# Feed-forward of a decoder layer: the three partial products of a block, ordered by part instead of by slice

## The chip, the cores and the metric

The kernel runs on one core of a Trainium2 chip. Its engines have queues of their own and meet by semaphores: TensorE (PE in the profile, PEld for its weight loads), VectorE (DVE), ScalarE (ACT), GpSimd (POOL) and SyncE (SP, which issues the DMAs). The metric is the device time of one execution in microseconds (us), as the median of the runs.

## The reference

One decoder layer on a sequence of 1024 tokens with width 1024. The change lies in its second half, the gated feed-forward:

```python
D_FF = -(-8 * D_MODEL // (3 * 256)) * 256          # 2816

def swiglu(h, w_gate, w_up, w_down):
    return (jax.nn.silu(h @ w_gate) * (h @ w_up)) @ w_down

def reference(...):
    ...
    x = layer_norm(ALPHA * x + gate1 * mix, ln1_g[l], ln1_b[l])
    h = x * (1.0 + scale2) + shift2
    ffn = swiglu(h, w_gate[l], w_up[l], w_down[l])
    x = layer_norm(ALPHA * x + gate2 * ffn, ln2_g[l], ln2_b[l])
    return x
```

All arrays are float32. The first half (modulation, projections, sparse attention, pooling, output projection, first norm) is the same in both kernels.

## The kernel before

**Numbers in two parts.** TensorE multiplies in a float32 form that rounds its operands. To keep precision, every operand is split into a high part (a rounded copy, made by ScalarE) and a low part (the operand less its high part, a subtraction on VectorE or GpSimd). A tile holds the high part in its columns 0 to 511 and the low part in 512 to 1023. A product of two operands is then three matmuls added up in PSUM, in the order of a table of pairs (part of the first operand, part of the second):

```python
SPLITS = ((0, 0), (0, 1), (1, 0))     # high by high, high by low, low by high
```

**Seven products in place of eight.** Each of the three feed-forward products of a pair of 128-column blocks is done as a two by two block product with seven block products (sums and differences of quarters are formed ahead, by GpSimd for weights and mostly by VectorE for activations). So gate, up and down consist of seven steps each. In `gu_step(kind, n, ...)` (`kind` "g" or "u", `n` 0 to 6) the weight block is the stationary operand and the tokens `TOK` (profile: `hr_H`) the moving one; the twelve matmuls of a step (four slices `k` by three pairs) accumulate in one PSUM bank, `gu`. In `down_step(p, n)` the activations `ACTS` (`act_W`, `act_R`) are stationary and the weight block moves; here the twelve matmuls are four row groups `i` by three pairs, and each row group has its own bank, `dn`, of the four banks of pool `ps3`.

**Weight blocks.** A block passes through GpSimd (sums, or a product with the gate row) in `wraw_R` or `wraw_W`, ScalarE (the high part) and VectorE or GpSimd (the low part) into one of four ring buffers: two in region V (`wblk_V`), two in region T (`wblk_T`). The raw sets come in by DMA; the next load is issued when a low part has been taken.

**Order.** The second half is written out by hand and kept in program order on TensorE, VectorE, ScalarE and GpSimd. A period `p` (1 to 9) has the steps of `DOWN_AT = 'dgggdggdggddduuduuuuu'`; below they are called d0 to d6, g0 to g6 and u0 to u6. So d3, d4 and d5 follow one another with nothing between them; all other down steps have gate or up steps in between. The last period has gate and up steps alone, and the last two down products are done by `last_down`.

**What is evacuated, and when.** The down step's banks are added to the residual (`res_X`) by four VectorE additions, one for each bank, right behind the step in VectorE's queue (`adds`). A table says which step begins new banks and which goes on in the banks of the step before (d1 in d0's, d3 in d2's, d5 in d4's; the additions take the bank's sum both times):

```python
DOWN = (("A11", "B11", True, (22,)), ("A12", "B21", False, (11,)), ("S1", "T1", True, (22,)), ("A22", "T4", False, (-21,)),
        ("S3", "T3", True, (22,)), ("S4", "B22", False, (-12,)), ("S2", "T2", True, (22,)))
```

New or not, a step's first matmul into a bank comes after the addition that read this bank before. In period 1 the first step's banks are copied by ScalarE and d1, d3 and d5 use a scaled addition in place of the plain one.

All engine calls go through one helper, so nearly every row of the profile says L174; the rows are told apart by their tiles.

Of the kernel before, what the change touches and what calls it, by code (L numbers as in the profile page):

```python
# [73 lines left out]
def f_(ap):  # L74

    return ap.bitcast(F32)


class Times:
# [11 lines left out]
    def place(self, ap):  # L91
        if ap.name in self.prev or ap.name in self.psum:
            p = self.psum.setdefault(ap.name, [np.zeros(2), np.full(2, " "), np.zeros(2), np.full(2, " ")])
            o = ap.offset % 1024
            return p, slice(o // 512, (o + ap.shape[-1] - 1) // 512 + 1) if len(ap.shape) == 2 else slice(0, 2)
        rng = getattr(ap.tensor, "manual_sbuf_range", None)
        if rng is None:
            return None
        es = {F32: 4, F32R: 4, I32: 4}.get(ap.dtype, 2)
        dims = list(ap.ap)  # L100
        lo = ap.offset % dims[0][0] if dims[0][0] else ap.offset
        hi = lo
        for st, n in dims[1:]:
            if st < 0:
                lo += st * (n - 1)
            else:
                hi += st * (n - 1)
        g = self.GRAIN
        return self.sbuf, slice((rng[0] + es * lo) // g, (rng[0] + es * hi) // g + 1)
# [77 lines left out]
def decoder_layer_kernel(  # L187
# [30 lines left out]
    def ps_tile(pool, tag, n, depth, nm):  # L218
        n_ps[0] += 1
        t = pool.tile([P, n], F32, tag=tag, name=f"{nm}_{n_ps[0]}")  # L220
        ring = ps_ring[tag]
        times.prev[t[:, 0:n].name] = ring[-depth] if len(ring) >= depth else None
        ring.append(t[:, 0:n].name)
        return t

    def psA(nm="pa"):
        return ps_tile(ps1, "ps1", 512, 4, nm)
# [65 lines left out]
    SPLITS = ((0, 0), (0, 1), (1, 0))  # L293
# [826 lines left out]
    for n_, u in enumerate(units):  # L1120
        g, pr, i = u
# [171 lines left out]
    def block(n):  # L1293
        if n < 8:
            return FIRST[n]
        if n < len(blocks) - 8 or n >= len(blocks) - 4:
            return RING[n % NRING]
        return TOK[:, 1, n + 8 - len(blocks)]
# [96 lines left out]
    def gu_step(kind, n, i0, ni, act, halves=True, turned=0):  # L1395


        gu_blk[n] = pos["used"] + (n if i0 + ni < 4 else n == 4 and halves)
        j = slice(i0 * P, (i0 + ni) * P)
        if n in (0, 1, 3):  # L1400
            gu_bank["ADxB"[n]] = psA("gu")[:, 0 : ni * P]
        banks = dict(gu_bank)
        ps_ = banks["ADABAAD"[n]]

        def mm(out_, m_, ks, new):
            w_, b = block(gu_blk[m_]), STEPS[m_][1]
            pv = out_.rearrange("p (i q) -> p i q", q=P)
            for k in ks:
                for m, (x, y) in enumerate(SPLITS):
                    T.matmul(pv, w_[:, x * 512 + k * P : x * 512 + (k + 1) * P], TOK[:, i0 : i0 + ni, b, y * 512 + k * P : y * 512 + (k + 1) * P],  # L1410
                             start=(new and k == 0 and m == 0), stop=(k == 3 and m == 2), skip_group_check=True)

        mm(ps_, n, range(2 if n == 3 and halves else 4), n in (0, 1, 3))
        if n == 4 and halves:
            mm(banks["B"], 3, (2, 3), False)

        gt = [GTMP[3 * turned], GTMP[1], GTMP[2], GTMP[3 - 3 * turned]]
        t1, t2, t4 = (x[:, j] for x in ((gt[0], gt[1], gt[3]) if kind == "g" else UTMP))
        outs = {4: ((3, t4), (0, t1)), 5: ((1, ps_),), 6: ((2, t2),)}.get(n, ())
        place = lambda q: gt[(0, 2, 1, 3)[q]]  # L1420
        sl = Slot()
        sl.used = ((1, 1, 1, 0, 2, 1, 1)[n] if halves else 1) if i0 + ni == 4 else 0

        def copy():
            if n in (0, 2, 4):
                A.activation((t1, None, t2, None, t4)[n], ps_, AF.Copy)

        def vec():
            for q, val in outs:
                if n == 4:  # L1430
                    V.tensor_tensor(val, val, banks["D" if q == 3 else "B"], ALU.add)
                elif n == 6:
                    V.tensor_tensor(val, val, ps_, ALU.add)
                if kind == "u":
                    V.tensor_tensor(place(q)[:, j], place(q)[:, j], val, ALU.mult)
            if kind == "u" and n == 5 and type(act) is dict:
                V.tensor_tensor(UTMP[0], place(1), place(3), ALU.add)

        def high(nm_, src):
            x = act[nm_]  # L1440
            A.activation(x[:, 0:512], src, AF.Copy)
            pend_low.append(lambda: (G if nm_ in ACT_G else V).tensor_tensor(x[:, 512:1024], src, f_(x[:, 0:512]), ALU.subtract))

        def sums():
            if kind == "u" and type(act) is dict:
                g11, g12, g21, g22 = gt
                todo_ = {5: (("S3", UTMP[2], g11, g21),), 6: (("S2", UTMP[0], UTMP[0], g11), ("S4", UTMP[1], UTMP[0], g12))}.get(n, ())
                for nm_, dst, x, y in todo_:
                    (G if nm_ in SUM_G else V).tensor_tensor(dst, x, y, ALU.subtract)
                    pend_high.append(lambda nm_=nm_, dst=dst: high(nm_, dst))  # L1450

        def act_():
            for q, val in outs:
                if kind == "g":
                    A.activation(place(q)[:, j], val, AF.Silu)
                elif type(act) is list:
                    high(q, place(q))
                elif q == 1:
                    high("S1", UTMP[0])
                else:  # L1460
                    high({0: "A11", 2: "A12", 3: "A22"}[q], place(q))

        sl.copy, sl.vec, sl.sums, sl.act = copy, vec, sums, act_
        return sl
# [64 lines left out]
    def E(rc, i):  # L1529

        t = 7 - 2 * i if rc >= 20 else 6 - 2 * i
        return XR[t][:, 0:512] if rc % 10 == 1 else XR[t][:, 512:1024]
# [176 lines left out]
    def down_step(p, n):  # L1709
        a_, w_, new, (to,) = DOWN[n]  # L1710
        wd_ = block(pos["used"])
        if new:
            bank.update({i: ps_tile(ps3, "ps3", 512, 4, "dn") for i in range(4)})
        banks = dict(bank)
        for i in range(4):
            for m, (a, b) in enumerate(SPLITS):
                T.matmul(banks[i], ACTS[a_][:, a * 512 + i * P : a * 512 + (i + 1) * P], wd_[:, b * 512 : (b + 1) * 512],
                         start=(new and m == 0), stop=(m == 2), skip_group_check=True)
        sl = Slot()
        sl.used = 1  # L1720

        def adds():
            for i in range(4):
                z = E(abs(to), i)
                if p == 0 and n == 0:
                    A.activation(z, banks[i], AF.Copy)
                elif p == 0 and not new:
                    V.scalar_tensor_tensor(z, z, float(np.float32(ALPHA)), banks[i], ALU.mult, ALU.add if to > 0 else ALU.subtract)
                else:
                    V.tensor_tensor(z, z, banks[i], ALU.add if to > 0 else ALU.subtract)  # L1730

        sl.copy = adds
        return sl
# [147 lines left out]
```

## Time and profile before

| | |
|---|---|
| median of 3 runs | 1268.83 us (1268.32 to 1272.6) |
| the profiled execution, its own time | 1269.91 us |
| its span, first to last instruction | 1268.1 us |
| mean granted TensorE clock | 0.977 |
| busy: PE / PEld / DVE / ACT / POOL | 94% / 73% / 79% / 52% / 56% |
| the down steps of periods 1 to 9 in the trace | from 639.48 us on, the last before `last_down` at 1155.6 us |
| share of PE in the chain that ended last | 67% |

Matmul rows show the latency of one (389 ns for 512 columns), which overlaps with the next; the pace of a stream is read from starts of successive rows. In a timeline, a row merges neighbours on an engine: its first number is the start, the second the length, `xN` the count, and the bracket the idle time ahead of it with what ended it.

### The profile page before, as it was taken

To read this page: it belongs to the slowest core of one execution; us is meant where nothing else is said; L and a number is where in the kernel's file an instruction comes from. 1 tells how busy PE (TensorE), PEld (TensorE's weight loads), DVE (VectorE), ACT (ScalarE), POOL (GpSimd) and SP (SyncE) were. 2 spreads that over 40 slices of the span, in tenths; PEclk is the share of its full clock that TensorE was granted. 3 is DMA by queue.
4 is the path that set the end of the run, shared out by engine and by line. 5 is a ranking of instruction groups with operands and counts; after the bars stand their busy time and mean duration, and the time that the engine had idled before them with its cause. 6 is when DMAs were issued, how large, how long until landed. Compare 5 with 4: busy or idle time off the path is not lost.

```text
span 1268.1 us, 16420 instructions
## 1 busy us (share of the span) xinstructions
PE 1197.6 (94%) x5622; PEld 930.9 (73%) x5622; DVE 998.7 (79%) x1842; ACT 662.4 (52%) x1351; POOL 709.3 (56%) x505
## 2 busy tenths in 40 slices
PE   7999999999998999996899999999999999999996
PEld 6766566677656667885778787887878787878775
DVE  6799997988898765776886878787777768687698
ACT  4667877887685894455443333243333333333531
POOL 0193474675032464285783848384756647486848
PEclk8999999999897999998999999999999999999998
DMA  9610167401000044100202111101112121212112
GB/s 348 244 50 17 62 249 272 154 39 59 17 9 9 26 166 165 61 9 22 103 26 84 34 67 34 67 34 67 48 53 67 34 83 34 84 34 100 57 61 116
DMA packets 32459, 103.40 MB, mean 82 GB/s; under 512 B 3572, under 2 KB 3572, under 8 KB 28792
## 3 DMA queue, kind: packets, MB, share of 16 engines
q1 hardware_dynamic: 32376, 102.36, 22.9%
q8 instruction: 44, 0.72, 0.2%
q14 instruction: 39, 0.32, 0.1%
HBM read 92.90 MB, written 9.45 MB: 81 GB/s over the span
## 4 chain that ended last, share of the span: by engine, by line
PE 67%; DVE 14%; POOL 6%; ACT 6%; issue 5%; DMA 1%; SPq 0%; DVEq 0%; POOLq 0%; ACTq 0%
PE gu L174 25%; PE dn L174 15%; PE pj L174 7%; PE wo L174 4%; PE pair L174 3%; PE pT L174 3%; PE s L174 2%; PE iq L174 2%; DVE act_W L174 2%; PE o L174 2%; POOL wraw_R L174 2%; PE lg L174 1%; DVE stat_C L174 1%; DVE utmp_X L174 1%; DVE junk_X L174 1%
## 5 line engine op out<-in xcount | busy, mean ns | idle before, releaser
L174 PE MATMUL gu<-hr_H,wblk_T 128*128 128x512 f32 (+1 forms) x924 | 217.5, 388 | 6.2 <-ACT gtmp_V L174 2.7
L174 PE MATMUL gu<-hr_H,wblk_V 128*128 128x512 f32 (+1 forms) x924 | 215.2, 385 | 3.6 <-POOL wblk_V L174 1.8
L174 PEld LDWEIGHTS gu<-hr_H,wblk_T 128*128 128x128 f32 x924 | 172.2, 191 | 42.4 <-POOL wblk_T L174 3.6
L174 PEld LDWEIGHTS gu<-hr_H,wblk_V 128*128 128x128 f32 x924 | 170.1, 188 | 39.8 <-POOL wblk_V L174 3.5
L174 DVE TENSOR_TENSOR res_X<-res_X,dn 128x512 f32<-128x512 f32 (+1 forms) x253 | 158.9, 677 | 15.4 <-PE dn L174 15.3
L174 POOL TENSOR_TENSOR wraw_R<-wraw_R 128x512 f32<-128x512 f32 x64 | 94.6, 1485 | 47.0 <-DVE wblk_T L174 23.7
L174 POOL TENSOR_TENSOR wraw_W<-wraw_W 128x512 f32<-128x512 f32 x60 | 86.7, 1452 | 58.0 <-DVE wblk_V L174 29.3
L174 PE MATMUL pj<-ws_W,hT_H 128*128 128x512 f32 x456 | 116.2, 400 | 1.4 <-DVE const_C L174 0.8
L174 POOL TENSOR_SCALAR sm_H<-sm_H,stat_X 128x1024 f32<-128x1024 f32 (+7 forms) x64 | 48.8, 776 | 116.3 <-DVE stat_X L174 80.5
L174 PEld LDWEIGHTS pj<-ws_W,hT_H 128*128 128x128 f32 x456 | 83.0, 188 | 25.2 <-issue 6.5
L174 PE MATMUL dn<-wblk_T,act_W 128*128 128x512 f32 x324 | 80.4, 398 | 4.6 <-DVE act_W L174 4.6
L174 PE MATMUL dn<-wblk_V,act_W 128*128 128x512 f32 x324 | 78.6, 392 | 2.9 <-DVE act_W L174 2.5
L174 DVE TENSOR_SCALAR_CACHE_REDUCE junk_X<-keysD_T,colsD_X 128x1024 int16<-128x1024 int16 (+1 forms) x64 | 79.4, 1268 | 0.2
L174 ACT ACTIVATE wblk_V<-wraw_R 128x512 fp32r<-128x512 f32 x56 | 35.2, 629 | 80.7 <-POOL wraw_R L174 62.2
L174 PEld LDWEIGHTS dn<-wblk_T,act_W 128*128 128x128 f32 x324 | 61.5, 191 | 19.5 <-DVE act_W L174 6.7
L174 PEld LDWEIGHTS dn<-wblk_V,act_W 128*128 128x128 f32 x324 | 60.4, 188 | 17.4 <-DVE act_W L174 4.2
L174 ACT ACTIVATE wblk_V<-wraw_W 128x512 fp32r<-128x512 f32 x53 | 33.1, 627 | 75.1 <-POOL wraw_W L174 56.4
L174 ACT ACTIVATE wblk_T<-wraw_W 128x512 fp32r<-128x512 f32 x56 | 35.0, 628 | 66.2 <-POOL wraw_W L174 50.1
L174 ACT ACTIVATE wblk_T<-wraw_R 128x512 fp32r<-128x512 f32 x52 | 32.5, 627 | 61.1 <-POOL wraw_R L174 45.6
L174 ACT ACTIVATE utmp_X<-gu 128x512 f32<-128x512 f32 x33 | 19.7, 598 | 73.4 <-PE gu L174 73.4
L174 DVE SCALAR_TENSOR_TENSOR score_X<-relu_K,const_C,score_X 128x384 f32<-128x384 f32 (+5 forms) x42 | 54.2, 1290 | 5.0 <-ACT relu_K L174 1.4
L174 ACT ACTIVATE junkA_T<-keys_T,colsA_X 128x768 bf16<-128x768 uint16 (+3 forms) x62 | 54.4, 877 | 3.8 <-DVE colsA_X L174 2.9
(299 smaller groups left out, 2745.9 us busy)
## 6 DMA issues: line engine op xcount, KB each, us to landing
mset_K<-in_wmr_dram SPq DMA_DIRECT2D x16, 1024.0 KB, 5.1
wm_K<-in_wma_dram SPq DMA_DIRECT2D x16, 512.0 KB, 10.0
wraw_R<-in_wg_dram SPq DMA_DIRECT2D x6, 1024.0 KB, 4.8
wraw_R<-in_wd_dram SPq DMA_DIRECT2D x12, 512.0 KB, 3.6
wraw_W<-in_wup_dram SPq DMA_DIRECT2D x12, 512.0 KB, 3.6
wraw_R<-in_wup_dram SPq DMA_DIRECT2D x10, 512.0 KB, 3.6
wraw_W<-in_wg_dram SPq DMA_DIRECT2D x5, 1024.0 KB, 4.8
wraw_W<-in_wd_dram SPq DMA_DIRECT2D x10, 512.0 KB, 3.5
```

The source lines that it names most:

```text
L174: ins_ = f(*a, **k)
```

## The change

Two loops are turned inside out. In a gate or up step the four slices `k` of the high-by-high product come first, then the four that need the low part of the tokens, then the four that need the low part of the weights. In a down step the four row groups (four banks) of the high-by-high product come first, then the four with the low part of the weights, then the four with the low part of the activations.

```diff
         def mm(out_, m_, ks, new):
...
-            for k in ks:
-                for m, (x, y) in enumerate(SPLITS):
+            for m, (x, y) in enumerate(SPLITS):
+                for k in ks:
                     T.matmul(pv, w_[:, x * 512 + k * P : x * 512 + (k + 1) * P], TOK[:, i0 : i0 + ni, b, y * 512 + k * P : y * 512 + (k + 1) * P],
                              start=(new and k == 0 and m == 0), stop=(k == 3 and m == 2), skip_group_check=True)
...
-        for i in range(4):
-            for m, (a, b) in enumerate(SPLITS):
+        for m, (a, b) in enumerate(SPLITS):
+            for i in range(4):
                 T.matmul(banks[i], ACTS[a_][:, a * 512 + i * P : a * 512 + (i + 1) * P], wd_[:, b * 512 : (b + 1) * 512],
                          start=(new and m == 0), stop=(m == 2), skip_group_check=True)
```

The number and shapes of all instructions stay, and only TensorE's queue is in another order; the queues of VectorE, ScalarE, GpSimd and SyncE read the same in both kernels. `last_down` and everything ahead of the feed-forward are untouched.

**A gate step on TensorE, before** (period 1, g2; `gu` is the bank, `hr_H` the tokens, `wblk_V` the weight block; the brackets say whose semaphores a row waits for):

```order
L174 MATMUL gu_5434<-hr_H_2748,wblk_V_4222 128x512 [waits DVE_49]
L174 MATMUL gu_5434<-hr_H_2748,wblk_V_4222 128x512 x9
L174 MATMUL gu_5414<-hr_H_2748,wblk_V_4223 128x512 [waits Activation_49]
L174 MATMUL gu_5414<-hr_H_2748,wblk_V_4223 128x512
L174 MATMUL gu_5414<-hr_H_2748,wblk_V_4223 128x512 [waits Pool_49]
L174 MATMUL gu_5414<-hr_H_2748,wblk_V_4223 128x512 x9
```

The same place on TensorE after:

```order
L174 MATMUL gu_5434<-hr_H_2748,wblk_V_4222 128x512 [waits DVE_49]
L174 MATMUL gu_5434<-hr_H_2748,wblk_V_4222 128x512 x3
L174 MATMUL gu_5414<-hr_H_2748,wblk_V_4223 128x512 [waits Activation_49]
L174 MATMUL gu_5414<-hr_H_2748,wblk_V_4223 128x512 x7
L174 MATMUL gu_5414<-hr_H_2748,wblk_V_4223 128x512 [waits Pool_49]
L174 MATMUL gu_5414<-hr_H_2748,wblk_V_4223 128x512 x3
```

The wait for the block's low part (here from GpSimd) stood at the third matmul of the step and stands at the ninth now.

**From d3 to d4 on TensorE, before** (period 1; `dn_5522` to `dn_5525` are the four banks of d2 and d3, `dn_5599` to `dn_5602` those of d4 and d5):

```order
L174 MATMUL dn_5525<-wblk_V_4222,act_W_4235 128x512 [waits DVE_49]
L174 MATMUL dn_5525<-wblk_V_4222,act_W_4235 128x512 x2
L174 MATMUL dn_5599<-wblk_V_4223,act_W_4238 128x512 [waits DVE_49,Activation_49]
L174 MATMUL dn_5599<-wblk_V_4223,act_W_4238 128x512 x2
L174 MATMUL dn_5600<-wblk_V_4223,act_W_4238 128x512 [waits DVE_49]
L174 MATMUL dn_5600<-wblk_V_4223,act_W_4238 128x512 x2
L174 MATMUL dn_5601<-wblk_V_4223,act_W_4238 128x512 [waits DVE_49]
L174 MATMUL dn_5601<-wblk_V_4223,act_W_4238 128x512 x2
```

The same place after:

```order
L174 MATMUL dn_5524<-wblk_V_4222,act_W_4235 128x512
L174 MATMUL dn_5525<-wblk_V_4222,act_W_4235 128x512
L174 MATMUL dn_5599<-wblk_V_4223,act_W_4238 128x512 [waits DVE_49,Activation_49]
L174 MATMUL dn_5600<-wblk_V_4223,act_W_4238 128x512 [waits DVE_49]
L174 MATMUL dn_5601<-wblk_V_4223,act_W_4238 128x512 [waits DVE_49]
L174 MATMUL dn_5602<-wblk_V_4223,act_W_4238 128x512 [waits DVE_49]
```

Each bank's first matmul waits for VectorE's addition of that bank, before and after. Before, these four waits stood three matmuls apart and so did the four banks' last matmuls; now both stand one matmul apart, the last matmuls of d3 right ahead of the waiting ones of d4.

## The prediction, as made before the run

> **What bounds the kernel now.** I read the page's busy line and costliest groups first, then busy time by stretch, then TensorE's own waits, and last the timeline of the down steps.
>
> ```profile
> PE 1197.6 (94%) x5622; PEld 930.9 (73%) x5622; DVE 998.7 (79%) x1842; ACT 662.4 (52%) x1351; POOL 709.3 (56%) x505
> ...
> L174 PE MATMUL gu<-hr_H,wblk_T 128*128 128x512 f32 (+1 forms) x924 | 217.5, 388 | 6.2 <-ACT gtmp_V L174 2.7
> L174 PE MATMUL gu<-hr_H,wblk_V 128*128 128x512 f32 (+1 forms) x924 | 215.2, 385 | 3.6 <-POOL wblk_V L174 1.8
> ...
> L174 PE MATMUL dn<-wblk_T,act_W 128*128 128x512 f32 x324 | 80.4, 398 | 4.6 <-DVE act_W L174 4.6
> ```
>
> ```profile
> 760.00:818.90 58.90, 57.80 (x254) 47.21 (x253) 44.62 (x62) 21.56 (x38) 36.52 (x26) 1.00 0.16 54
> ```
>
> The columns of the second fence are the stretch, its length, then busy PE, PEld, DVE, ACT and POOL, the clock, and DMA. This is one period of the feed-forward: TensorE is busy 57.8 of 58.9 us, VectorE 44.6. So TensorE's queue is the bound, only what moves its waits counts, and VectorE has 14 us of air in a period.
>
> ```profile
> PE dn L174 <- DVE act_W L174: 7.1, 9, 2.0
> PE gu L174 <- POOL wblk_T L174: 1.9, 4, 0.5
> PE gu L174 <- POOL wblk_V L174: 1.8, 4, 0.5
> PE gu L174 <- DVE wblk_T L174: 1.5, 1, 1.5
> PE gu L174 <- DVE wblk_V L174: 1.1, 1, 1.1
> PE dn L174 <- DVE res_X L174: 0.4, 1, 0.4
> ```
>
> (Total us, times, longest.) The first five rows are waits for low parts, 13.4 us in all, which the new order can relieve. The last row is the wait for an addition that reads a bank: 0.4 us in the whole kernel, so this is hidden now.
>
> **The gain: low parts needed later.** Two waits come back in each period. Period 3, TensorE, and the work that it waits for:
>
> ```profile
> 760.02 0.61 PE L174 MATMUL dn<-wblk_V,act_W 128*128 128x512 f32 x2
> 761.27 2.58 PE L174 MATMUL dn<-wblk_V,act_W 128*128 128x512 f32 x10 [0.63 <-DVE act_W L174]
> 763.68 2.88 PE L174 MATMUL gu<-hr_H,wblk_V 128*128 128x512 f32 x12
> 766.40 3.34 PE L174 MATMUL gu<-hr_H,wblk_T 128*128 128x512 f32 x14
> 770.21 2.57 PE L174 MATMUL gu<-hr_H,wblk_T 128*128 128x512 f32 x10 [0.47 <-POOL wblk_T L174]
> 772.62 0.62 PE L174 MATMUL dn<-wblk_V,act_W 128*128 128x512 f32 x2
> ...
> 758.83 2.38 DVE L174 TENSOR_TENSOR act_W<-gtmp_V,act_W 128x512 fp32r<-128x512 f32 x2
> ...
> 768.87 1.29 POOL L174 TENSOR_TENSOR wblk_T<-wraw_W,wblk_T 128x512 fp32r<-128x512 f32 x1
> ```
>
> An undisturbed step takes 766.40 - 763.68 = 2.72 us, 0.227 for each of twelve matmuls. d0 starts at 760.02 and g0 follows at 763.68: 3.66 - 2.72 = 0.94 lost. It stops at its third matmul until the low part of `act_W` ends at 761.21; the matmul starts 0.06 later, and the ten left take 2.41 in place of 2.27, so a wait also costs 0.14 of refill. In the new order that part is needed by the ninth matmul, at 760.02 + 8 x 0.227 = 761.84, after it is ready: 0.94 gained in each of periods 2 to 9, 7.5 us.
>
> g2 starts twelve matmuls into the x14 row, at 769.12, and loses 772.62 - 769.12 - 2.72 = 0.78. It would start 0.94 sooner, at 768.18, since d0 no longer stops; its ninth matmul comes at 770.00, and GpSimd's low part ends at 770.16. GpSimd doesn't come forward with TensorE: its rows hang on VectorE's work behind the last up step. So 0.22 + 0.14 = 0.36 is left and 0.42 gained, 3.4 us in eight periods (0 to 0.78 each for the range).
>
> Period 1 has the long wait, and a slow clock behind it:
>
> ```profile
> 639.48 0.62 PE L174 MATMUL dn<-wblk_T,act_W 128*128 128x512 f32 x2
> 642.13 4.14 PE L174 MATMUL dn<-wblk_T,act_W 128*128 128x512 f32 x10 [2.03 <-DVE act_W L174]
> 646.11 1.08 PE L174 MATMUL gu<-hr_H,wblk_T 128*128 128x512 f32 x4
> ...
> 615.20:618.60 3.40, 1.58 (x12) 1.49 (x12) 2.38 (x4) 1.94 (x4) 2.10 (x3) 1.00 0.00 0
> 618.60:622.00 3.40, 3.23 (x20) 2.85 (x20) 3.40 (x5) 1.02 (x3) 3.40 (x3) 1.00 0.00 0
> 639.10:642.50 3.40, 1.37 (x7) 0.82 (x6) 3.40 (x5) 0.94 (x2) 1.64 (x1) 1.00 0.00 0
> 642.50:645.90 3.40, 3.40 (x10) 2.63 (x9) 3.33 (x6) 0.22 (x1) 1.21 (x1) 0.50 0.00 0
> ```
>
> This d0 loses 646.11 - 639.48 - 2.72 = 3.91. In the new order it stops only at 639.48 + 1.82 = 641.30, until 642.13: 0.83 + 0.14 = 0.97 stays, and the stretch before 642.5 is then busy enough that I take the 0.50 clock to go. Gain 2.9 (1.4 if the clock stays). The single wait on VectorE's `wblk_V` (1.1 us, with the latency tail and refill 1.4) is in the last period, whose end waits for VectorE anyway: I take half, 0.7. The one for `wblk_T` (1.5) is ahead of period 1, with longer waits behind it: nothing, at most 1.5. Gains together: 7.5 + 3.4 + 2.9 + 0.7 = 14.5 us.
>
> **The cost: four banks end together.** The place is d3, d4, d5, in period 3:
>
> ```profile
> 788.93 5.60 PE L174 MATMUL dn<-wblk_T,act_W 128*128 128x512 f32 x24
> 794.38 2.88 PE L174 MATMUL dn<-wblk_V,act_W 128*128 128x512 f32 x12
> 797.10 2.88 PE L174 MATMUL gu<-hr_H,wblk_V 128*128 128x512 f32 x12
> ...
> 789.74 0.68 DVE L174 TENSOR_TENSOR wblk_V<-wraw_R,wblk_V 128x512 fp32r<-128x512 f32 x1
> 790.35 4.92 DVE L174 TENSOR_TENSOR res_X<-res_X,dn 128x512 f32<-128x512 f32 x8
> 795.18 0.69 DVE L174 TENSOR_TENSOR wblk_T<-wraw_W,wblk_T 128x512 fp32r<-128x512 f32 x1
> 795.78 2.47 DVE L174 TENSOR_TENSOR res_X<-res_X,dn 128x512 f32<-128x512 f32 x4
> ...
> 802.53 1.75 PE L174 MATMUL dn<-wblk_T,act_W 128*128 128x512 f32 x7
> 803.41 0.69 DVE L174 TENSOR_TENSOR res_X<-res_X,dn 128x512 f32<-128x512 f32 x1 [1.56 <-PE dn L174]
> ```
>
> Today d3 to d5 run without a gap (8.17 us). An addition takes 0.68 and follows the next at (2.47 - 0.68) / 3 = 0.60; a bank is finished every three matmuls, 0.68, so VectorE keeps up beside TensorE. The last two rows give the handover: the third matmul of d6 ends at 802.53 + 0.45 + 0.39 = 803.37, the addition starts 0.04 later.
>
> In the new order, counted from d3's start: bank 0 gets its last matmul as the ninth, done at 1.82 + 0.39 = 2.21, so the additions start at 2.25 (VectorE is free at 1.49) and end at 2.93, 3.53, 4.13, 4.73. d4 could start at 2.72, but its first four matmuls each need one of these: 2.99, 3.59, 4.19, 4.79. The other eight follow with the refill: d4 ends at 4.79 + 0.23 + 0.14 + 1.82 = 6.97 in place of 5.45. The same once more: bank 0 of d4 is done at 6.45, the additions end at 7.17 to 8.97, d5's first four start at 7.23 to 9.03, and u0 follows at 11.22 in place of 8.17. **3.05 us in each period.** Both steps wait on the same thing: four additions at 0.60 against four matmuls at 0.227.
>
> That neighbouring matmuls go to different banks costs nothing by itself: the end of the output projection does it too (slices, pairs, then two banks in turn), and there eighteen take 4.37 us, which less one latency of 0.39 and the refill of 0.14 behind its wait is 0.226 for each of seventeen.
>
> ```profile
> 576.70 4.37 PE L174 MATMUL wo<-hr_H,plT_T 128*128 128x512 f32 x18
> ```
>
> Other down steps are safe: a gate or up step stands behind each, and the banks are needed again 5 us later or more. What comes late next is VectorE: d5's additions end 3.9 later than now against TensorE's 3.05, d6's 1.4 later. The low parts queued behind them have these idle times as cover, 1.53 and 1.98 us:
>
> ```profile
> 801.16 0.69 DVE L174 TENSOR_TENSOR wblk_V<-wraw_W,wblk_V 128x512 fp32r<-128x512 f32 x1 [1.53 <-ACT wblk_V L174]
> 809.33 0.69 DVE L174 TENSOR_TENSOR wblk_V<-wraw_W,wblk_V 128x512 fp32r<-128x512 f32 x1 [1.98 <-ACT wblk_V L174]
> ```
>
> So I cost it at nothing (0.85 a period if the cover fails). Period 1 has such a wait already (the 0.4 above; 0.6 with tail and refill): 2.4 more there. Cost: 8 x 3.05 + 2.4 = 26.8 us.
>
> **Sum.** 26.8 - 14.5 = +12.3 us on the profiled execution's own 1269.91, which is 1.1 above the median of 1268.83: about 1281. Low end: every low-part wait goes (8 x 1.72 + 3.9 + 1.4 + 1.5 = 20.6) and no refill is paid (8 x 2.77 + 1.8 = 24.0): +3.4, 1272. High end: 0.85 more a period (33.6) and only d0's waits gained (7.5 + 1.4): +24.7, 1294.
>
> **Rivals.**
> *The banks don't hold TensorE (faster).* Then only the gains stay: 1254. It decides if d3's last addition ends 1.3 us sooner, at 3.40 where the waiting matmul would stand undisturbed. For it speaks that this wait is 0.4 us today; against, that the additions' pace is measured at 0.60 and that VectorE can't start before a bank is finished. 6%.
> *The two cancel (within 0.5%, 1262.5 to 1275, about what a measurement of this kernel can tell from no change).* While TensorE stands in d4 and d5, the others gain 3 us of lead on it, so that nothing is left of g2's wait and of those ahead; with the low end's sums about 1273. Against: g2's wait hangs on the last up step, behind the stall. 12%.
> *The clock falls in the sparse stretches (much slower).* The rows show 0.50 after a stretch with 1.37 of 3.40 us busy and none after one with 1.58. A new sparse stretch has four matmuls of 0.39 in 2.4 us, with 1 us of full work about 2.5 busy: above both. If it falls all the same, 3.4 us at half clock lose 1.7: one for each of 18 stretches 31 us, 1312; one in four, 1289. 12%.
> The Trainium skill speaks for this one: "TensorE: Matmul & The Clock Gate", in the section on psum-queue depth-cycling, tells of a kernel whose TensorE idled briefly between groups as it cycled banks and whose clock swung between half and full. By that rule the sum is the 1312, and here the trace's 615 row speaks against it.
>
> **Numbers.** Forecast 70%, and 12, 12 and 6 for the rivals. Slower 0.81 (forecast less its low tail, and the clock), same 0.13, faster 0.06. The range 1273 to 1292 takes in the forecast's ends nearly whole and the mild clock case.
>
> **What would show it.** d3 to d5 go from 8.2 to about 11.2 us; the wait for `res_X` additions grows from 0.4 to some 13 us (the gaps between latencies, 72 times); `act_W` waits all but vanish, GpSimd's shrink to short ones; a period goes from 58.85 to about 60.5. Wrong would be: d4's first four matmuls still 0.227 apart, VectorE's low parts ending a wait in u2 or u3, or clock rows of 0.50 beyond 646.

## The result and the profile after

The changed kernel takes 1287.17 us (median of 4 runs, 1286.26 to 1287.9) against 1269.16 for the kernel before in the same comparison: a ratio of 1.0132 with a 95% interval of 1.0119 to 1.0145, so 1.3% slower. The forecast was 1281, in a range of 1273 to 1292. The profiled execution's own time is 1286.26 us and its span 1284.5, both 16.4 us more than before; the sum had said 12.3.

The page's busy line and the groups that answer to those shown before, with VectorE's additions beside them (the last column is idle time ahead of the group and what ended it):

```profile
PE 1215.0 (95%) x5622; PEld 928.8 (72%) x5622; DVE 1000.7 (78%) x1842; ACT 661.8 (52%) x1351; POOL 709.0 (55%) x505
...
L174 PE MATMUL gu<-hr_H,wblk_T 128*128 128x512 f32 (+1 forms) x924 | 217.2, 387 | 5.0 <-ACT gtmp_V L174 4.0
...
L174 DVE TENSOR_TENSOR res_X<-res_X,dn 128x512 f32<-128x512 f32 (+1 forms) x253 | 157.0, 676 | 52.6 <-PE dn L174 52.6
...
L174 PE MATMUL dn<-wblk_T,act_W 128*128 128x512 f32 x324 | 86.7, 402 | 5.0 <-DVE res_X L174 2.2
L174 PE MATMUL dn<-wblk_V,act_W 128*128 128x512 f32 x324 | 86.4, 402 | 4.3 <-DVE res_X L174 2.3
```

TensorE is "busier" than before, 1215.0 us in place of 1197.6, with the same 5622 matmuls. The 17 us more are no work: the row of a matmul that waits for its bank is longer (the four of d4 in period 3 are 0.47 to 0.50 us long, the others 0.39 to 0.40), so most of the 0.60 from one such matmul to the next is counted as busy. Of the 11.34 us that d3 to d5 take in period 3 (below), 10.37 are busy. VectorE's side shows the stall: its additions stood idle 52.6 us for the down banks. Before, it was 15.4:

```profile
L174 DVE TENSOR_TENSOR res_X<-res_X,dn 128x512 f32<-128x512 f32 (+1 forms) x253 | 158.9, 677 | 15.4 <-PE dn L174 15.3
```

TensorE's own waits:

```profile
PE gu L174 <- ACT gtmp_V L174: 8.8, 6, 2.1
PE dn L174 <- DVE res_X L174: 4.4, 18, 0.3
...
PE gu L174 <- DVE wblk_T L174: 0.8, 1, 0.8
PE dn L174 <- DVE act_W L174: 0.7, 1, 0.7
```

The low parts are gone from the list but for the last two rows, and a wait for `res_X` has come up 18 times, twice in each of nine periods.

Period 3 in the timeline, TensorE and then VectorE, where d0 starts at 763.32 and d3 at 790.92:

```profile
763.32 2.88 PE L174 MATMUL dn<-wblk_V,act_W 128*128 128x512 f32 x12
766.04 2.88 PE L174 MATMUL gu<-hr_H,wblk_V 128*128 128x512 f32 x12
768.76 5.94 PE L174 MATMUL gu<-hr_H,wblk_T 128*128 128x512 f32 x24
774.54 1.76 PE L174 MATMUL dn<-wblk_V,act_W 128*128 128x512 f32 x7
...
790.92 2.91 PE L174 MATMUL dn<-wblk_T,act_W 128*128 128x512 f32 x12
794.15 4.06 PE L174 MATMUL dn<-wblk_T,act_W 128*128 128x512 f32 x12 [0.32 <-DVE res_X L174]
798.38 4.04 PE L174 MATMUL dn<-wblk_V,act_W 128*128 128x512 f32 x12 [0.17 <-DVE res_X L174]
802.26 1.07 PE L174 MATMUL gu<-hr_H,wblk_V 128*128 128x512 f32 x4
...
824.02 2.20 PE L174 MATMUL dn<-wblk_V,act_W 128*128 128x512 f32 x9
...
792.73 0.68 DVE L174 TENSOR_TENSOR wblk_V<-wraw_R,wblk_V 128x512 fp32r<-128x512 f32 x1
793.33 2.47 DVE L174 TENSOR_TENSOR res_X<-res_X,dn 128x512 f32<-128x512 f32 x4
797.54 2.48 DVE L174 TENSOR_TENSOR res_X<-res_X,dn 128x512 f32<-128x512 f32 x4 [1.75 <-PE dn L174]
```

d0 runs through in 2.72 us (it took 3.66); g1 and g2 together lose 774.54 - 768.76 - 5.44 = 0.34. d3 to u0 takes 802.26 - 790.92 = 11.34 in place of 8.17, and VectorE now stops for TensorE between d3's and d4's additions, and TensorE for VectorE behind each. The period is 824.02 - 763.32 = 60.70 us, before 58.84 (760.02 to 818.86).

### The profile page after: what moved, and what is told of

It is laid out like the page before. It is cut to its first block, busy times and chain, and to the rows that moved or that the text cites. A ratio compares the mean times of both kernels' runs of the same rounds, so it can differ in the third digit from the quotient of the medians.

```text
span 1284.5 us, 16420 instructions
## 1 busy us (share of the span) xinstructions
PE 1215.0 (95%) x5622; PEld 928.8 (72%) x5622; DVE 1000.7 (78%) x1842; ACT 661.8 (52%) x1351; POOL 709.0 (55%) x505
## 4 chain that ended last, share of the span: by engine, by line
PE 51%; DVE 19%; POOL 15%; issue 7%; ACT 6%; DMA 1%; SPq 0%; DVEq 0%; POOLq 0%; ACTq 0%
PE gu L174 16%; PE dn L174 8%; PE pj L174 7%; POOL wraw_R L174 5%; POOL wraw_W L174 4%; PE wo L174 4%; DVE res_X L174 3%; PE pair L174 3%; PE pT L174 2%; PE s L174 2%; PE iq L174 2%; DVE act_W L174 2%; PE o L174 2%; DVE utmp_X L174 2%; POOL wblk_T L174 1%
## 5 line engine op out<-in xcount | busy, mean ns | idle before, releaser
L174 DVE TENSOR_TENSOR res_X<-res_X,dn 128x512 f32<-128x512 f32 (+1 forms) x253 | 157.0, 676 | 52.6 <-PE dn L174 52.6
L174 PE MATMUL dn<-wblk_T,act_W 128*128 128x512 f32 x324 | 86.7, 402 | 5.0 <-DVE res_X L174 2.2
L174 PE MATMUL dn<-wblk_V,act_W 128*128 128x512 f32 x324 | 86.4, 402 | 4.3 <-DVE res_X L174 2.3
```

The source lines that it names most:

```text
L174: ins_ = f(*a, **k)
```

## The experiments

### Gate and up steps alone, and down steps alone

The first kernel (gate half) takes the upper part of the diff alone, the second (down half) the lower part alone, each on the kernel before.

```diff
-            for k in ks:
-                for m, (x, y) in enumerate(SPLITS):
+            for m, (x, y) in enumerate(SPLITS):
+                for k in ks:
...
-        for i in range(4):
-            for m, (a, b) in enumerate(SPLITS):
+        for m, (a, b) in enumerate(SPLITS):
+            for i in range(4):
```

> Gate and up steps in the new order, down steps in the old one. Theory (all the loss is made by the banks of d3, d4 and d5; a gate step in the new order only gains): g2 no longer stops for its weights' low part (0.78 us a period, needed 1.36 us later now), eight periods 6.2 us; d0 still loses its 0.94; the wait of 1.4 us in the last period is replaced by the one for ScalarE that stands behind it. About 1263 us. Rival (the new order of the gate steps is itself part of the loss, because low parts of the tokens and weights alternate in another way): 1269 or more.

> Down steps in the new order, gate and up steps in the old one. Theory: 3.18 us lost in d3 to d5 of each period (2.4 in period 1), and d0's 0.94 are not gained but handed to g2, which now comes 0.94 sooner and waits that much longer for GpSimd at its third matmul; period 1 keeps about 0.9. 1269 + 27 = about 1296 us. Rival (the gains of d0 and g2 are independent): d0's 7.5 us stay, about 1289.

Measured: the gate half 1265.51 us, ratio 0.9961 (0.9947 to 0.9975), 5 us faster than its comparison's 1270.62, where 6 were expected. The down half 1298.52 us, ratio 1.022 (1.0205 to 1.0236), 28 us slower, where 27 were expected. So the gate half is a gain and the down half makes the whole loss, and more than the change as a whole. The rivals of both expectations (the new order of the gate steps is part of the loss, 1269 or more; the two gains are independent, 1289) fall. Where d0's gain went when the gate steps are old is in this timeline of the down half, TensorE, period 3:

```profile
773.66 3.33 PE L174 MATMUL gu<-hr_H,wblk_T 128*128 128x512 f32 x14
778.39 2.60 PE L174 MATMUL gu<-hr_H,wblk_T 128*128 128x512 f32 x10 [1.40 <-POOL wblk_T L174]
```

g2's wait at its third matmul, 0.47 us idle before, is 1.40 now: the 0.94 that d0 no longer loses. GpSimd's low part does not come sooner.

### The old order back in d3, d4 and d5, and the new order there alone

On the changed kernel:

```diff
-        for m, (a, b) in enumerate(SPLITS):
-            for i in range(4):
+        for i, m in ([(i, m) for i in range(4) for m in range(3)] if n in (3, 4, 5) else
+                     [(i, m) for m in range(3) for i in range(4)]):
+            a, b = SPLITS[m]
```

The counterpart, on the kernel before, has the two lists the other way round.

> The new order everywhere except in d3, d4 and d5, which keep the old one (a bank is finished before the next is begun). Theory: d3 to d5 run without a gap again (8.2 us from d3 to u0) and the gains of d0 (0.94) and g2 (0.42) stay, eight periods 10.9 us, 0.9 in period 1: about 1257 us, faster than both kernels. Rival (additions that come later, in d5 and d6 as well, delay the low parts behind them in VectorE's queue and so the whole period): no better than half way, 1275 or more.

> The new order in d3, d4 and d5 alone; all else as before. Theory: 3.18 us in each of eight periods and 2.4 in period 1 are added and nothing is gained, since d0 and g2 wait for work that hangs on the last up step: 1269 + 27 = about 1296 us. Rival (while TensorE stands in d4 and d5 the other engines get ahead, and the waits of d0 and g2, 1.7 us a period, shrink or go): 1283 to 1290.

Measured: with the old order back in the three steps 1265.24 us, ratio 0.9962 (0.9949 to 0.9975); with the new order there alone 1297.12 us, ratio 1.021 (1.0195 to 1.0225). The loss lies in these three steps: putting them back takes the changed kernel from 1287 to below the kernel before, and they alone cost 26.5 us of the 27 expected. The rival of the second expectation (1283 to 1290) falls. The three steps in the second of these kernels:

```profile
794.75 2.88 PE L174 MATMUL dn<-wblk_T,act_W 128*128 128x512 f32 x12
797.82 4.03 PE L174 MATMUL dn<-wblk_T,act_W 128*128 128x512 f32 x12 [0.19 <-DVE res_X L174]
802.05 4.02 PE L174 MATMUL dn<-wblk_V,act_W 128*128 128x512 f32 x12 [0.19 <-DVE res_X L174]
805.90 1.30 PE L174 MATMUL gu<-hr_H,wblk_V 128*128 128x512 f32 x5
```

They take 11.15 us, 2.98 more than before, where the working had 3.05.

The expectation for the first was 1257, and 8 us of that did not come. The same place there:

```profile
788.39 0.39 PE L174 MATMUL dn<-wblk_T,act_W 128*128 128x512 f32 x1
789.18 2.12 PE L174 MATMUL dn<-wblk_T,act_W 128*128 128x512 f32 x8 [0.40 <-POOL wblk_T L174]
...
787.84 1.29 POOL L174 TENSOR_TENSOR wblk_T<-wraw_R,wblk_T 128x512 fp32r<-128x512 f32 x1
```

d3 in the old order needs the low part of its weights at the second matmul, and GpSimd ends it at 789.13. TensorE is 1.3 us ahead by then (d3 starts 27.60 us behind d0, 28.91 before) and loses 0.79 - 0.23 = 0.56 there, 0.7 with the refill, in each of eight periods: 5.6 us. So half of what d0 and g2 gain is lost again at the next low part. The profiled execution also has two stretches at half clock that the changed kernel's has not (last section). One lies in period 1: from g2's start to d1's it is 4.45 us in place of 2.86, 1.6 lost. The other lies ahead of it, from 618.4 us on: from the first gate matmul to d0 of period 1 it is 59.96 us in place of 58.57, 1.4 lost. The three make 8.6 us, about what is missing; only the first of them comes from the edit. The rival (late additions hold up the whole period, 1275 or more) falls.

### Half an addition

In the changed kernel, VectorE's plain additions behind d3 and d4 take 256 of 512 columns; the other half of these sums is missing from the residual. Nothing is changed on TensorE.

```diff
                 else:
-                    V.tensor_tensor(z, z, banks[i], ALU.add if to > 0 else ALU.subtract)
+                    c = 256 if n in (3, 4) else 512
+                    V.tensor_tensor(z[:, 0:c], z[:, 0:c], banks[i][:, 0:c], ALU.add if to > 0 else ALU.subtract)
```

> The changed kernel, but VectorE's additions behind d3 and d4 of periods 2 to 9 take 256 of the 512 columns (the other half of these sums is left out of the residual). Theory (four additions at 0.60 us against four matmuls at 0.227 hold TensorE): an addition of half the columns takes 0.41 us (the shortest row of this kind before) and, as an estimate, 0.33 us of pace; d3 to d5 then lose 1.1 us in place of 3.18, 2.1 a period, 17 us: about 1270. Rival (it is the waiting itself that costs, four handovers between TensorE and VectorE in a row, not the additions' length): stays at 1284 or more.

Measured: 1268.79 us, ratio to the kernel before 0.9994 (0.9985 to 1.0004), so 18 us of the changed kernel's loss are gone, as expected. TensorE and VectorE in period 3:

```profile
785.80 6.19 PE L174 MATMUL dn<-wblk_T,act_W 128*128 128x512 f32 x24
791.92 3.25 PE L174 MATMUL dn<-wblk_V,act_W 128*128 128x512 f32 x12
795.01 1.30 PE L174 MATMUL gu<-hr_H,wblk_V 128*128 128x512 f32 x5
...
788.21 1.40 DVE L174 TENSOR_TENSOR res_X<-res_X,dn 128x256 f32<-128x256 f32 x4
791.35 1.42 DVE L174 TENSOR_TENSOR res_X<-res_X,dn 128x256 f32<-128x256 f32 x4 [1.75 <-PE dn L174]
```

Four additions take 1.40 us, a pace of 0.33 each, and d3 to u0 takes 9.21: 1.04 above 8.17, expected 1.1. The number of handovers is the same, so it is the additions' length that holds TensorE, not the waiting.

### Up steps between the down steps

```diff
-DOWN_AT = 'dgggdggdggddduuduuuuu'
+DOWN_AT = 'dgggdggdggdudududuuuu'
```

On the changed kernel (all products in the new order), and as a control on the kernel before.

> The changed kernel with one more edit: up steps between the down steps (d3 u0 d4 u1 d5 u2 d6), so each bank has 2.7 us more before it is used again. Theory (the loss is the reuse of four banks right behind their common end): VectorE's additions end 2.2 to 2.8 us behind a step's end at the latest, so nothing is lost in d3 to d5 and the gains of d0 and g2 stay: 1287 - 9 x 3.18 = about 1258 us, if the moved steps cost nothing elsewhere. Rival (later additions in VectorE's queue delay the low parts behind them): still above 1275.

> The kernel before with the same spread of the down steps (d3 u0 d4 u1 d5 u2 d6), all products in the old order. Theory: no bank wait was there to take away, so the spread alone changes nothing: 1269, within 4 us. Rival (the spread is better or worse by itself, through loads, low parts or VectorE's queue): off by more than that, and the spread kernel with the new order is to be read against this one.

Measured: with the new order 1262.26 us, ratio 0.9945 (0.9932 to 0.9958); with the old order 1270.09 us, ratio 0.9999 (0.9990 to 1.0008). The spread does nothing by itself and takes 25 us from the changed kernel: with 2.7 us between a step's end and the banks' next use, the bunching costs little. It is 4 us above the 1258 expected, and its timeline (TensorE from d3 to d5, then VectorE) shows most of the reason:

```profile
785.88 2.88 PE L174 MATMUL dn<-wblk_T,act_W 128*128 128x512 f32 x12
788.60 2.88 PE L174 MATMUL gu<-hr_H,wblk_T 128*128 128x512 f32 x12
791.32 3.32 PE L174 MATMUL dn<-wblk_V,act_W 128*128 128x512 f32 x12
794.48 2.88 PE L174 MATMUL gu<-hr_H,wblk_V 128*128 128x512 f32 x12
...
788.47 1.39 DVE L174 TENSOR_TENSOR wblk_V<-wraw_R,wblk_V 128x512 fp32r<-128x512 f32 x1
789.78 2.47 DVE L174 TENSOR_TENSOR res_X<-res_X,dn 128x512 f32<-128x512 f32 x4
```

d4 takes 794.48 - 791.32 = 3.16, 0.44 too much: d3's additions start only at 789.78, behind a low part in VectorE's queue, and the last of them ends at 792.25, when d4's fourth matmul would stand at 792.00. Eight times 0.44 is 3.5 us. The expectation had VectorE free sooner. In the profiled execution the end behind period 9 is also 1.7 us longer (97.91 us in place of the changed kernel's 96.21), where the expectation had put the moved steps' cost elsewhere at nothing.

### A mixed order in d3

As the kernel with the old order in d3 to d5, but d3 takes the four high products first and the other two pairs bank by bank.

```diff
+        for i, m in ([(i, 0) for i in range(4)] + [(i, m) for i in range(4) for m in (1, 2)] if n == 3 else
+                     [(i, m) for i in range(4) for m in range(3)] if n in (4, 5) else
                      [(i, m) for m in range(3) for i in range(4)]):
```

> As the kernel with the old order in d3, d4 and d5 and the new one elsewhere, but d3 takes its four high products first and then the other two pairs bank by bank. d3 now needs its weights' low part at the fifth matmul in place of the second (0.68 us later), so the 0.70 a period lost there should go. Theory (GpSimd's low part for d3 ended that gain): VectorE is free 2.41 us behind d3's start, so d4's first matmul waits 0.4 and pays a refill; about 0.2 us a period better, 1.5 us in all: about 1264. Rival (GpSimd's chain is the only limit): all 0.70 come back, 1259 to 1260.

Measured: 1263.32 us, ratio 0.9951 (0.9938 to 0.9964), by the ratios 1.4 us below the kernel that it is made from, with intervals that overlap: this step alone is not shown by the time. Its timeline tells more:

```profile
785.67 2.93 PE L174 MATMUL dn<-wblk_T,act_W 128*128 128x512 f32 x12
788.93 2.99 PE L174 MATMUL dn<-wblk_T,act_W 128*128 128x512 f32 x12 [0.33 <-DVE res_X L174]
791.76 2.88 PE L174 MATMUL dn<-wblk_V,act_W 128*128 128x512 f32 x12
```

The wait for GpSimd's low part is gone from d3, and a wait for VectorE's first addition stands at d4 (3.26 from d3's start to d4's, 0.54 lost, then 0.11 of refill). This speaks against the rival that GpSimd's chain is the only limit. Of the versions run, this one and the spread have the lowest medians, 0.5% below the kernel before; by their times, these two, the gate half and the kernel with the old order in d3 to d5 can't be told apart.

The length of a period tells them apart better, since the clock stays at 1.00 in periods 2 to 9 of all ten profiles. It is taken here from the start of d0 in period 2 to the first matmul of the last period, divided by eight:

| kernel | from, us | to, us | one period, us |
|---|---|---|---|
| before | 701.20 | 1171.94 | 58.84 |
| changed | 702.60 | 1188.27 | 60.71 |
| gate half | 698.99 | 1164.94 | 58.24 |
| down half | 706.35 | 1201.29 | 61.87 |
| old order back in d3 to d5 | 702.52 | 1168.48 | 58.25 |
| new order in d3 to d5 alone | 704.00 | 1198.66 | 61.83 |
| half additions | 699.66 | 1168.31 | 58.58 |
| mixed order in d3 | 699.91 | 1165.16 | 58.16 |
| spread, new order | 700.31 | 1164.17 | 57.98 |
| spread, old order | 701.21 | 1171.95 | 58.84 |

So the mixed order gains 0.09 us a period, where 0.2 were expected, the spread in the new order has the shortest period, and the spread in the old order changes nothing.

## Why the prediction was right, and where its sizes were off

**The bound and the cost.** That TensorE's queue is the bound, and that d3, d4 and d5 hold it through their banks, came out as worked: the old order there took the loss away, the new order there alone made all of it, and halving the additions cut it to a third. The working's 3.05 us a period is 2.98 where nothing else is changed (the new order in these steps alone) and 11.34 - 8.17 = 3.17 in the changed kernel. The term mis-sized is "VectorE is free at 1.49", counted from d3's start: it held for a TensorE that is not ahead. In the changed kernel TensorE reaches d3 1.31 us sooner (27.60 us behind d0 in place of 28.91), the low part ahead of VectorE's additions comes only 0.31 sooner (29.41 in place of 29.72), and the additions start at 793.33 - 790.92 = 2.41 in place of 2.25. About 0.15 a period, a bit over 1 us. What was put at nothing, the low parts behind VectorE's later additions, cost at most 0.1 a period: a period grew by 60.71 - 58.84 = 1.87, and 3.17 less the gains of d0 and g2 is 1.79.

**The gain at d0 and g2.** 0.94 and 0.42 a period were forecast. d0 loses nothing now, and 0.34 is left at g2 (forecast 0.36), so 0.44 is gained there. The down half alone shows that the two are one chain, as the working had it.

**Period 1.** This is the largest miss. d0 itself went as forecast: it stops once, and the half clock behind it is gone. But the gain of 2.9 was given back two steps later:

```profile
642.08 1.20 PE L174 MATMUL dn<-wblk_T,act_W 128*128 128x512 f32 x4 [0.73 <-DVE act_W L174]
643.11 2.89 PE L174 MATMUL gu<-hr_H,wblk_T 128*128 128x512 f32 x12
645.84 2.88 PE L174 MATMUL gu<-hr_H,wblk_V 128*128 128x512 f32 x12
650.49 3.02 PE L174 MATMUL gu<-hr_H,wblk_V 128*128 128x512 f32 x12 [1.77 <-ACT gtmp_V L174]
...
649.83 0.61 ACT L174 ACTIVATE gtmp_V<-gu 128x512 f32<-128x512 f32 x1
```

g2 goes on in a bank that ScalarE must first copy, and this copy stands in ScalarE's queue behind other work that did not move (the four copies of d0's banks start at 647.92, before at 647.96). From d0's start to d1's it is 13.98 us in place of 14.80: 0.8 stays of 2.9, so 2.1 us are missing. That the clock stayed at 1.00 behind this wait is in part luck (last section). I had asked what is late next for VectorE and GpSimd, not for ScalarE.

**The last period.** I took half of 1.4. TensorE there stops for ScalarE's copy instead, and nothing is left (0.7 missing): from the last period's first matmul to the end it is 96.21 us, before 96.19.

```profile
1198.88 1.45 PE L174 MATMUL gu<-hr_H,wblk_T 128*128 128x512 f32 x5 [0.92 <-ACT gtmp_V L174]
```

The working makes a period 58.85 - 0.94 - 0.42 + 3.05 = 60.54. Together 2.1 + 0.7 + 8 x (60.70 - 60.54) = 4.1 us, the difference between 12.3 and 16.4.

**The rivals.** *The banks don't hold TensorE* is ruled out by the new order in d3 to d5 alone and by the half additions. *The two cancel* fails because the others do not get ahead while TensorE stands: with the stall alone, the waits at d0 and g2 stay in full (1.02 and 0.89 us between the starts around them; 1.02 and 0.86 before). *The clock falls* did not happen: in the changed kernel the clock stayed at 1.00 from 656 to 1250 us. Here are the stretch across d3 and d4 of period 4 and the one behind it. The busy time was 2.8 us where I had estimated 2.5, since the waiting rows are longer than 0.39.

```profile
854.00:857.40 3.40, 2.83 (x10) 1.37 (x9) 2.51 (x5) 0.81 (x2) 2.55 (x2) 1.00 0.00 0
857.40:860.80 3.40, 2.97 (x11) 1.47 (x9) 2.54 (x5) 0.63 (x1) 0.00 (x0) 1.00 0.00 0
```

What the Trainium skill tells of a kernel that cycles banks ("TensorE: Matmul & The Clock Gate", psum-queue depth-cycling), a clock that swings, did not come here: the idle time listed ahead of d4 and d5 is at most 0.34 us, and the clock stayed.

**The signs named.** d3 to d5 at 11.2 (11.34 with the step behind it), the period at 60.5 (60.70) and the vanished `act_W` waits came as said. The wait for `res_X` is 4.4 us in the list, not 13, and 18 times, not 72: the list has the first of four waits. The others show as longer rows (0.50 in place of 0.39) with 0.10 us between them or less, which the list leaves out.

## What to carry to other kernels

An order that needs its late operands last also finishes all its accumulators last. Where the next group reuses them at once, compare the evacuation's pace with the matmul's (here 0.60 to 0.227 us): the difference is paid for every bank, and an independent step in between hides most of it. A wait taken away brings TensorE forward, and the engines that feed it hardly (1.31 to 0.31 us here), so the gain is worth what the next late operand leaves of it, on every engine of the chain.

## What the runs showed of the hardware

The prediction took the clock to fall after a stretch with 1.37 of 3.40 us busy and not after 1.58. That is no threshold. The kernel with the old order in d3 to d5 has the same wait in period 1 as the changed kernel, g2's for ScalarE's copy, with 2.16 us between the matmul starts around it in both. There the clock fell to 0.50 behind it; in the changed kernel it stayed. Busy time by stretch, in the same columns as in the prediction; the first fence is the former kernel, the second the latter:

```profile
649.10:652.50 3.40, 1.63 (x7) 1.05 (x6) 2.15 (x2) 3.40 (x8) 3.40 (x3) 1.00 0.00 0
652.50:655.90 3.40, 3.40 (x9) 2.63 (x8) 2.83 (x2) 1.02 (x2) 3.40 (x3) 0.50 0.00 0
```

```profile
649.20:652.60 3.40, 2.11 (x9) 1.76 (x10) 1.60 (x2) 3.32 (x7) 3.40 (x4) 1.00 0.00 0
652.60:656.00 3.40, 3.40 (x17) 2.82 (x16) 2.29 (x2) 0.00 (x0) 3.40 (x4) 1.00 0.00 0
```

In the first it lies within one of the stretches of 3.4 us at whose ends the clock changes, with 1.63 us busy, and in the second it reaches over an end, with 2.11. The mixed order in d3, whose TensorE queue is the same up to d3, has the gap over an end too, 2.11 us between starts and 2.11 busy, and the clock stayed. So where a gap lies decides as well as its length.

The prediction's row at 615 was itself on the edge. The kernel with the spread in the old order has the same rows there, 0.12 us earlier, and in its profile the clock fell behind them:

```profile
615.05:618.45 3.40, 1.55 (x12) 1.48 (x12) 2.36 (x4) 1.94 (x4) 2.10 (x3) 1.00 0.00 0
618.45:621.85 3.40, 3.23 (x15) 3.06 (x14) 3.40 (x5) 1.02 (x3) 3.40 (x3) 0.50 0.00 0
```

A few hundredths of a microsecond less busy cost 1.4 us: from the first gate matmul to d0 of period 1 it is 59.98 us in place of 58.57. The clock fell at this place in four of the ten profiles (the two halves, the old order back in d3 to d5, and this one). A difference of 1.4 to 1.6 us between two profiled executions can therefore be chance. Over all ten, every such stretch at full clock with less than 1.45 us busy was followed by 0.50 and none with more than 2.15; in between it went both ways, so busy time by rows is not the whole measure.

The Trainium skill ("TensorE: Matmul & The Clock Gate", What's actually happening) says that the clock's monitor looks at fixed windows of 3.4 us that run on by themselves; these traces agree: in the changed kernel's the clock is at 0.50 from 587.77 to 601.42 us, four times 3.41. The same page's advice (Why this matters for your kernels) is to have no idle gaps over some 3 us; here 1.77 us of idle time were enough (ahead of g2, in the kernel of the first fence).
